# A fused convolution and RWKV-7 block: depthwise taps at the lowest priority, x normalised two tiles at once, side work in one queue per slot, h loaded ahead, the chunk chain traced later, the adaLN gate computed in block 1

## The chip, the cores and the metric

The kernel runs on one core of a Trainium2 chip. A core has TensorE (PE in the profile; its weight loads are PEld), VectorE (DVE), ScalarE (ACT), GpSimd (POOL) and SyncE (SP), which here only issues DMAs. Each engine works through its own queue in order and meets the others at semaphores. The metric is the device time of one execution, in microseconds.

## The reference, cut to what matters

```python
mod = silu(c) @ ada_w + ada_b;  shift, scale, gate = split(mod, 3)
h = rmsnorm(x, norm_g) * (1 + scale) + shift                       # 2048 tokens x 1024
p = h @ w_in                                                       # 1024 x 9344, split in the next line
c_val, c_gate, c_og, ts, r_og, g_conv, g_rwkv = split(p)

u = c_val * sigmoid(c_gate)
u = causal_depthwise_conv(u, conv_k, width=31) + conv_b            # per channel, along the tokens
y_conv = (silu(layernorm(u)) * silu(c_og)) @ w_conv_out

r, k, v, w_low, a_low = split(token_shift(ts, mu))                 # 16 heads of 64
decay, a = f(w_low @ w2), sigmoid(a0 + a_low @ a2)
for t in tokens:                                                   # per head, state S is 64 x 64
    S = S * decay[t] - (S @ kk[t]) b[t]^T + v[t] k[t]^T;  o[t] = S @ r[t]
o = groupnorm(o) + sum(r * k * r_k) * v
y_rwkv = (o * silu(r_og)) @ w_rwkv_out

m = sigmoid(g_conv) * y_conv + sigmoid(g_rwkv) * y_rwkv
out = rmsnorm(x + gate * (m @ w_out), final_g)
```

All is float32. `gate` enters only at the end; `shift` and `scale` are needed for the first h.

## The kernel before

The 2048 tokens are worked in four blocks of 512 (b = 0 to 3). Channels lie on partitions. A projection is one 128-channel tile of `w_in`: `mm3` makes it of 24 matmuls (8 slices of D, and three products each of the high and low parts of weight and h, since a float32 is split in two parts for PE's faster float32 form). These matmuls, at L180, are called main matmuls. A block projects 73 such tiles: one for the low-rank parts (`lora_split`) and then 18 in each of four slots. A slot (b, g) belongs to group g, which is two pairs of heads times two, 256 channels: `slot` projects k, r, v for each pair, and between and after them convolution and gate tiles (`fill`). 432 main matmuls make a slot.

Beside this stream run side tasks, written as Python generators. A task's `yield a, b` says that what it just emitted takes PE a us and that it goes on b us later; `tick` counts 0.684 us for every three main matmuls and polls the tasks. So PE's order, which is kept as written (`manual_schedule`), has the tasks' matmuls at planned places between main matmuls. `drain` lets the planned time run on without main matmuls until a task is done. The other engines' queues and SP's are ordered by the Tile scheduler from a simulated timeline, with priorities (`tc.high_priority`); its order is fixed in the program. The tasks are:

- `pair`: for one pair, decay, the chunk matrices `KR`, `BK`, the masked products `As` (PE L569, mask on DVE L572 and L579), transposes `tk`.
- `group`: when both pairs of a slot have their `As`, the 64x64 triangles are inverted: 32x32 quarters go out by DMA (`dA`, `La`), POOL does 62 small operations (L653, L655: "the inverse"), the result comes back (`dT`), DVE transposes quarters (L687), PE makes the lower and upper quarters (L700, L704). Then the chunk chain: 8 chunks of 64 tokens with three PE steps each (L757, then DVE `Xz`; L766, then DVE `uv`; L782, then the state `S` on DVE, L786). Then the group norm (DVE L803 to L811, POOL L805 and L812, ACT L808), and for each pair four PE transposes (L819) into the one PSUM bank `late`, which ACT empties (`oc`, L821). The chain of slot g runs while slot g+1 projects.
- `taps`: the 31 taps of one convolution tile on DVE (L861, L866), summed in one PSUM bank.
- `xnorm`: token tiles (128 tokens) of x for the next block: squares on ACT, a reciprocal root by some ten 128x1 operations on DVE (`rsqrt`, L109 to L114), x scaled (L365), transposed on PE (L371), modulated on ACT and stored as `xT_dram`. `XN` says which tiles a slot takes: here one in slot 0, one in slot 1, two in slot 2.

`hprep` reads h of the next block from `xT_dram`, tile by tile, and splits it in a high (ACT L384) and a low part (DVE L385). `presplit` splits a half tile of `w_out` (named "o": row gate from DRAM, multiplied on POOL, L144) or of `w_rwkv_out` ("ro") in two parts (ACT L145, POOL L146) and stores them; four such halves are emitted at the start of each slot of blocks 1 (w_out) and 2 (w_rwkv_out). The gate column is made after slot (0,0) by eight loads of 512 KB and DVE products (`ada_cols`, L200, L201), and its row goes to DRAM (L1039). Small tiles of all these share seven buffers, `hx`. In block 3 the LayerNorm of block 0 (`lnorm_first`) is done in three parts. After the blocks follow the output projections, block by block, with LayerNorm and final norm (L1087 to L1209).

## Time and profile before

| what | us |
|---|---|
| median of 3 runs (lowest, highest) | 3078.06 (3073.18, 3084.10) |
| the profiled execution, its own time | 3076.14 |
| its span, first to last instruction | 3074.4 |
| TensorE matmul, busy in the span | 2806.0 |
| VectorE, GpSimd, ScalarE busy | 2092.9, 1183.6, 1003.0 |

How to read it: `L371` is line 371 of the kernel before; `out<-in` are the names of the tiles an instruction writes and reads. In a list of waits stand the total us, how often, and the longest. In a window's row stand its length, each engine's busy us with the number of instructions (PE, PEld, DVE, ACT, POOL), the granted share of TensorE's clock, the DMA engines' busy share and GB/s. In a timeline, start and us, then the instruction, and in brackets how long the engine was idle before it and what ended that. In a list of groups, us in total and mean ns of one, then idle time before them.

### The profile page before, as it was taken

How to read it: one execution, taken by the hardware profiler on the slowest of the kernel's cores; microseconds unless marked ns; L12 is line 12 of the kernel's file. 1: busy time of each engine (PE TensorE's matmuls, PEld its weight loads, DVE VectorE, ACT ScalarE, POOL GpSimd, SP SyncE). 2: the span in 40 equal slices, each digit the busy share in tenths (PEclk: the TensorE clock that was granted, in tenths of full speed). 3: DMA queues.
4: the chain of work that ended last, by engine and by line, in shares of the span. 5: the costliest groups of instructions: out<-in, count | busy, mean ns of one | idle time of the engine just before them, and what ended most of it. 6: DMA issues, size and time to landing. Idle time of an engine off the chain costs nothing.

```text
span 3074.4 us, 50973 instructions
## 1 busy us (share of the span) xinstructions
PE 2806.0 (91%) x18640; PEld 2292.0 (75%) x18640; DVE 2092.9 (68%) x4279; ACT 1003.0 (33%) x1932; POOL 1183.6 (38%) x1742
## 2 busy tenths in 40 slices
...
GB/s 305 271 233 200 233 226 258 199 248 173 194 198 204 194 243 159 209 170 216 176 211 220 185 169 263 208 210 171 227 199 153 256 189 293 305 250 240 217 225 177
DMA packets 354795, 666.90 MB, mean 217 GB/s; under 512 B 134704, under 2 KB 153456, under 8 KB 354544
## 3 DMA queue, kind: packets, MB, share of 16 engines
...
q8 instruction: 147, 2.41, 0.3%
q14 instruction: 104, 0.85, 0.1%
HBM read 483.07 MB, written 179.31 MB: 215 GB/s over the span
## 4 chain that ended last, share of the span: by engine, by line
PE 40%; DVE 15%; DMA 8%; POOL 6%; issue 4%; SPq 2%; ACT 1%; POOLq 0%; DVEq 0%; ACTq 0%
PE ps_main L180 27%; DVE acc L866 5%; PE pout L1187 2%; PE pout L1186 2%; PE pout L1188 2%; DMA w_st<-w_ro_t 1%; POOL TT L655 1%; POOL itmp L653 1%; PE aux L569 1%; DMA w_gr<-grow_d 1%; PE xo L766 1%; SPq L666 1%; PE xo L740 1%; DVE S L786 1%; PE xo L782 1%
## 5 line engine op out<-in xcount | busy, mean ns | idle before, releaser
L180 PE MATMUL ps_main<-h_hi,w_hi 128*128 128x512 f32 x2304 | 966.3, 419 | 27.1 <-ACT w_hi L163 14.5
L180 PE MATMUL ps_main<-h_hi,w_lo 128*128 128x512 f32 x2304 | 918.9, 399 | 12.4 <-DMA w_lo<-kl_in 4.8
L180 PE MATMUL ps_main<-h_lo,w_hi 128*128 128x512 f32 x2304 | 915.6, 397 | 0.2 <-DVE h_lo L385 0.2
L866 DVE SCALAR_TENSOR_TENSOR acc<-u,ck,acc 128x512 f32<-128x512 f32 x928 | 697.9, 752 | 21.0
L180 PEld LDWEIGHTS ps_main<-h_hi,w_hi 128*128 128x128 f32 x2304 | 442.5, 192 | 121.5 <-ACT w_hi L163 16.4
L180 PEld LDWEIGHTS ps_main<-h_hi,w_lo 128*128 128x128 f32 x2304 | 440.2, 191 | 120.7 <-POOL w_lo L165 7.6
L180 PEld LDWEIGHTS ps_main<-h_lo,w_hi 128*128 128x128 f32 x2304 | 442.7, 192 | 80.1 <-DVE h_lo L385 1.4
L653 POOL TENSOR_TENSOR itmp<-La,TT 128x126 f32<-128x126 f32 (+22 forms) x496 | 181.9, 367 | 156.4 <-DMA La<-dA 120.5
L786 DVE SCALAR_TENSOR_TENSOR S<-xo,pe,Se 64x64 f32<-64x64 f32 x512 | 144.7, 283 | 141.9 <-PE xo L782 129.4
L163 ACT CAST w_hi<-w_st 128x1024 fp32r<-128x1024 f32 x103 | 108.0, 1048 | 307.2 <-DMA w_st<-w_in_t 128.1
L655 POOL TENSOR_TENSOR TT<-TT,itmp 128x126 f32<-128x126 f32 (+22 forms) x496 | 190.9, 385 | 35.3
L165 POOL TENSOR_TENSOR w_lo<-w_st,w_hi 128x1024 fp32r<-128x1024 f32 x50 | 120.5, 2409 | 133.0 <-ACT w_hi L163 58.2
L761 ACT ACTIVATE Se<-S,pe 128x128 f32<-128x128 f32 x256 | 89.0, 395 | 142.9 <-DVE S L786 141.9
L766 PEld LDWEIGHTS xo<-Xz,As 128*64 128x64 f32 x1024 | 69.6, 138 | 70.4 <-DVE Xz L762 38.4
L165 DVE TENSOR_TENSOR w_lo<-w_st,w_hi 128x1024 fp32r<-128x1024 f32 x53 | 70.5, 1331 | 68.0 <-PE ps_main L180 38.3
L572 DVE TENSOR_TENSOR As<-aux,maskA 128x512 f32<-128x512 f32 x128 | 82.7, 684 | 47.5 <-PE aux L569 47.0
L450 ACT ACTIVATE t<-ps_main,mu 128x512 f32<-128x512 f32 x96 | 65.9, 686 | 136.5 <-PE ps_main L180 133.9
L735 ACT COPY Xz<-xo 64x256 f32<-64x256 f32 x128 | 46.9, 367 | 189.4 <-PE xo L740 129.6
L766 PE MATMUL xo<-Xz,As 128*64 128x64 f32 x1024 | 87.4, 229 | 23.2 <-DVE Xz L762 23.0
L777 DVE TENSOR_TENSOR uv<-xo,rn 64x256 f32<-64x256 f32 x128 | 53.7, 419 | 80.3 <-PE xo L766 66.6
L847 POOL COPY u<-tail 128x30 f32<-128x30 f32 x32 | 10.2, 322 | 251.5 <-DVE yj L866 237.7
L762 DVE TENSOR_TENSOR Xz<-xo,Xz 64x256 f32<-64x256 f32 x128 | 53.7, 420 | 77.4 <-PE xo L757 75.8
...
## 6 DMA issues: line engine op xcount, KB each, us to landing
w_hi<-kh_in SPq DMA_DIRECT2D x219, 512.0 KB, 3.9
w_lo<-kl_in SPq DMA_DIRECT2D x219, 512.0 KB, 5.1
...
```

What stands on the lines that cost most here:

```text
L163: nc.scalar.copy(hi, st)
L165: lo_eng.tensor_tensor(out=lo, in0=st, in1=hi.bitcast(F32), op=ALU.subtract)
L180: nc.tensor.matmul(ps[:, qs], ww[:, k, :], aa[k][:, qs], start=(k == 0 and t == 0 and q == 0), stop=(k == KT - 1 and t == 2 and q == ms - ...
L450: nc.scalar.activation(t1, ps, AF.Identity, scale=mu1[:, mi:mi + 1])
L572: nc.vector.tensor_tensor(out=Asb[:, hh, c4 * 4:c4 * 4 + 4, :].rearrange("p (a e) n -> p a (e n)", e=2), in0=pA[hh], in1=flat(maskA).unsqu ...
L653: nc.gpsimd.tensor_tensor(out=tmp[:, :ni, :nt], in0=La[:, j:j + 1, j + 1:].broadcast_to([P, ni, nt]), in1=TT[:, :ni, j:j + 1].broadcast_to ...
L655: nc.gpsimd.tensor_tensor(out=TT[:, :ni, j + 1:], in0=TT[:, :ni, j + 1:], in1=tmp[:, :ni, :nt], op=ALU.add)
L761: nc.scalar.mul(Se[:, q, :], Sg[:, q, :], R[q]["pe"][:, c:c + 1])
L766: nc.tensor.matmul(b_[pr_, q, hs], As[q][:, hh, c, kcol(e)], Xz[:, e, q, hs], start=(n == 0), stop=(n == 3), skip_group_check=True)
L786: nc.vector.scalar_tensor_tensor(out=Sg[hs, q, hs], in0=b_[hs, 2 + q, hs], scalar=R[q]["pe"][hs, c:c + 1], in1=Se[hs, q, hs], op0=ALU.mult ...
L866: nc.vector.scalar_tensor_tensor(out=acc if i + 1 < HALO else yj, in0=u[:, i:i + TB], scalar=ck[:, j, i:i + 1], in1=acc, op0=ALU.mult, op1 ...
L1186: nc.tensor.matmul(o_, mhi[kk][:, ts_], whi[:, k, :], start=first, stop=False, skip_group_check=True)
```

## The change

- `taps`: each tap is emitted at a priority of -1500 (`LOWP`).
- `xnorm`: slot 0 takes two tiles, slot 1 the other two. Both tiles are loaded, squared and scaled first, their small DVE operations at high priority; after a longer planned delay (8 + 28 us for one tile's 18) follow the transposes.
- `sides`: one task per slot does, one after another, `xnorm`, then in slot (1,0) the gate (`gate_col`), in block 3 a part of the LayerNorm (`norms`), and in blocks 1 and 2 four presplits, 4 us apart. The list `later` is turned round: `w_rwkv_out` in block 1, `w_out` in block 2, since its row gate is made in block 1 now.
- `gate_col`: 16 loads of 256 KB into `hx` buffers, each with a DVE product, and the row to DRAM; `ada_cols` for the gate after slot (0,0) is gone.
- `hload`: h of the next block is loaded (seven tiles in `hx`, one in the buffer of `sq`) before the last three tiles of slot 3; `hprep` only splits.
- `pair` and `group` have longer planned delays: in `pair` 4.5 for 3.0, 6.0 for 4.5, 3.0 for 2.6; before the quarters 6.0 for 4.5; the chain's three steps 2.6 for 2.0, 2.5 for 2.0, 3.3 for 2.8; the norm, now at high priority, 30 for 18 us before its transposes.

```diff
@@ -45,9 +45,10 @@
-
-XN = ((0,), (1,), (2, 3), ())
+LOWP = 1500
+
+
+XN = ((0, 1), (2, 3), (), ())
 ZN = ((0, 1, 2), (3, 4, 5), (6, 7), ())
@@ -127,7 +128,7 @@
 
     kept = {}
 
-    later = [("o", (cb, kh)) for cb in range(4) for kh in range(2)] + [("ro", j) for j in range(KT)]
+    later = [("ro", j) for j in range(KT)] + [("o", (cb, kh)) for cb in range(4) for kh in range(2)]
...
 
     def xnorm(b, tts):
+        if not tts:
+            return
+        held = []
         for tt in tts:
...
             for half in range(2):
                 xt = hx("xt")
                 nc.sync.dma_start(xt, x[t0:t0 + P, half * TB:half * TB + TB])
-                nc.scalar.activation(hx("xsq"), xt, AF.Square, accum_out=ss[:, half:half + 1])
                 xh.append(xt)
+            for half in range(2):
+                nc.scalar.activation(hx("xsq"), xh[half], AF.Square, accum_out=ss[:, half:half + 1])
             vs, rs = ss[:, 2:3], ss[:, 3:4]
-            nc.vector.tensor_tensor(out=vs, in0=ss[:, 0:1], in1=ss[:, 1:2], op=ALU.add)
-            nc.vector.tensor_scalar(out=vs, in0=vs, scalar1=1.0 / D, scalar2=RMS_EPS, op0=ALU.mult, op1=ALU.add)
-            rsqrt(rs, vs, e2, nc.vector, ss[:, 4:5])
-            for kh in range(2):
-                nc.vector.tensor_scalar(out=xh[kh], in0=xh[kh], scalar1=rs, scalar2=None, op0=ALU.mult)
-            yield 0.0, 18.0
+            with tc.high_priority(HP):
+                nc.vector.tensor_tensor(out=vs, in0=ss[:, 0:1], in1=ss[:, 1:2], op=ALU.add)
+                nc.vector.tensor_scalar(out=vs, in0=vs, scalar1=1.0 / D, scalar2=RMS_EPS, op0=ALU.mult, op1=ALU.add)
+                rsqrt(rs, vs, e2, nc.vector, ss[:, 4:5])
+                for kh in range(2):
+                    nc.vector.tensor_scalar(out=xh[kh], in0=xh[kh], scalar1=rs, scalar2=None, op0=ALU.mult)
+            held.append((tt, xh))
+            yield 0.0, 8.0
+        yield 0.0, 28.0
+        for tt, xh in held:
             for kh in range(2):
                 yield free
                 pt = pl.tile([P, 4, P], F32, name="late", tag="late")
@@ -375,7 +384,7 @@
                     nc.scalar.activation(xo[:, i, :], pt[:, i, :], AF.Identity, scale=g_col[:, k:k + 1],
                                          bias=shift_col[:, k:k + 1])
                 nc.sync.dma_start(xT_dram[b][:, kh * 4:kh * 4 + 4, tt * P:(tt + 1) * P], xo)
-                yield 0.6, 3.5
+                yield 0.6, 4.5
 
...
 
-    def hprep(b):
+    def hload(b):
+        hfs = []
+        for k in range(KT):
+            hf = hx("hf") if k < HXB else e1.tile([P, TB], F32, name="hf", tag="sq")
+            nc.sync.dma_start(hf, xT_dram[b][:, k, :])
+            hfs.append(hf)
+        return hfs
+
+    def hprep(hfs):
         h = ([], [])
         for k in range(KT):
-            hf = hx("hf")
-            nc.sync.dma_start(hf, xT_dram[b][:, k, :])
-            hsplit(h, k, hf)
+            hsplit(h, k, hfs[k])
         return h
...
                                            scalar=vc("rwkv_k_k", pr), in1=E1x[:, :, e, :], op0=ALU.mult, op1=ALU.mult)
-        yield 0.0, 3.0
+        yield 0.0, 4.5
         yield free
...
-        yield 0.0, 4.5
+        yield 0.0, 6.0
...
-            yield 1.2, 2.6
+            yield 1.2, 3.0
...
-        yield 0.0, 4.5
+        yield 0.0, 6.0
...
-            yield 0.6, 2.0
+            yield 0.6, 2.6
...
-            yield 1.1, 2.0
+            yield 1.1, 2.5
...
-            yield 0.6, 2.8
+            yield 0.6, 3.3
...
-        yield 0.5, 18.0
+        with tc.high_priority(HP):
+            nc.vector.tensor_reduce(out=r4(st), in_=O16, axis=AX.X, op=ALU.add)
+            nc.vector.tensor_scalar(out=st, in0=st, scalar1=1.0 / 64, scalar2=None, op0=ALU.mult)
+            nc.gpsimd.tensor_tensor(out=O16, in0=O16, in1=bc(st), op=ALU.subtract)
+            for half in range(2):
+                Dm = lt.tile([P, 8, 64], F32, name="Dm", tag="oc", bufs=OCB)
+                nc.scalar.activation(Dm.rearrange("p (a b) n -> p a b n", a=2), O16[:, half * 2:half * 2 + 2], AF.Square)
+                nc.vector.tensor_reduce(out=st[:, half * 8:half * 8 + 8], in_=Dm, axis=AX.X, op=ALU.add)
+            nc.vector.tensor_scalar(out=st, in0=st, scalar1=1.0 / 64, scalar2=GN_EPS, op0=ALU.mult, op1=ALU.add)
+            rsqrt(rs, st, lt, nc.vector)
+            nc.gpsimd.tensor_tensor(out=O16, in0=O16, in1=bc(rs), op=ALU.mult)
+        yield 0.5, 30.0
...
-        nc.vector.tensor_scalar(out=acc, in0=u[:, HALO:], scalar1=ck[:, j, HALO:HALO + 1], scalar2=vc("conv_b", j),
-                                op0=ALU.mult, op1=ALU.add)
+        with tc.high_priority(-LOWP):
+            nc.vector.tensor_scalar(out=acc, in0=u[:, HALO:], scalar1=ck[:, j, HALO:HALO + 1], scalar2=vc("conv_b", j),
+                                    op0=ALU.mult, op1=ALU.add)
         for i in range(HALO):
             if i % 2:
                 yield 0.0, 2.0
-            nc.vector.scalar_tensor_tensor(out=acc if i + 1 < HALO else yj, in0=u[:, i:i + TB],
-                                           scalar=ck[:, j, i:i + 1], in1=acc, op0=ALU.mult, op1=ALU.add)
+            with tc.high_priority(-LOWP):
+                nc.vector.scalar_tensor_tensor(out=acc if i + 1 < HALO else yj, in0=u[:, i:i + TB],
+                                               scalar=ck[:, j, i:i + 1], in1=acc, op0=ALU.mult, op1=ALU.add)
...
-    def once(f):
-        yield free
-        f()
+    def gate_col():
+        sr = []
...
+        hg = e2.tile([P, 2, KT], F32, name="hg", tag="hg", bufs=1)
+        yield 0.0, 3.0
+        for k in range(KT):
+            for half in range(2):
+                st_ = hx("ada")
+                nc.sync.dma_start(st_, ada[16 + k][:, half * TB:half * TB + TB])
+                nc.vector.scalar_tensor_tensor(out=st_, in0=st_, scalar=1.0, in1=sr[half], op0=ALU.mult, op1=ALU.mult,
+                                               accum_out=hg[:, half, k:k + 1])
+            yield 0.0, 3.0
+        nc.vector.tensor_tensor(out=hgate_col, in0=hg[:, 0, :], in1=hg[:, 1, :], op=ALU.add)
+        nc.vector.tensor_tensor(out=hgate_col, in0=hgate_col, in1=ab[:, 16:24], op=ALU.add)
+        nc.vector.tensor_scalar(out=hgate_col, in0=hgate_col, scalar1=0.5, scalar2=None, op0=ALU.mult)
+        nc.sync.dma_start(grow_d.rearrange("(n p) -> p n", p=P), hgate_col)
+
+    def sides(b, g):
+        if b + 1 < NB:
+            yield from xnorm(b + 1, XN[g])
+        if b == 1 and g == 0:
+            yield from gate_col()
+        yield from norms(b, g)
+        if b in (1, 2):
+            for _ in range(2):
+                n_ = later.pop(0)
+                for half in range(2):
+                    presplit(*n_, half)
+                    yield 0.0, 4.0
+
+    def norms(b, g):
+        if b + 1 == NB and g < 3:
+            yield free
+            lnorm_first(g)
...
@@ -981,16 +1037,9 @@
         G = opened(b, g, h, lora)
         if first:
             G.wait = 8.0
-        if b in (1, 2):
-            for _ in range(2):
-                n_ = later.pop(0)
-                for half in range(2):
-                    presplit(*n_, half)
-        if b + 1 < NB:
-            side[:] = [Task(xnorm(b + 1, XN[g]))]
-        else:
+        side[:] = [Task(sides(b, g))]
+        if b + 1 == NB:
             z_first(ZN[g])
-            side[:] = [Task(once(lambda: lnorm_first(g)))] if g < 3 else []
...
+        if g < 3 or b + 1 == NB:
+            fill(len(todo))
+            return None
+        fill(len(todo) - 3)
+        drain(*side)
+        hfs = hload(b + 1)
         fill(len(todo))
+        return hfs
...
     with tc.manual_schedule(engines={mybir.EngineType.PE}):
         for b in range(NB):
             if b:
-                drain(*side)
-                h = hprep(b)
+                h = hprep(hfs)
             lora = lora_split(h)
             for g in groups:
-                slot(b, g, h, lora, g == 0)
-                if b == 0 and g == GG:
-                    for _ in ada_cols(srow, l3, "As", ASB, [((16 + k, 17 + k), (hgate_col[:, k:k + 1], hgate_col[:, k + 1:k + 2]))
-                                                            for k in range(0, KT, 2)]):
-                        pass
-                    nc.vector.tensor_tensor(out=hgate_col, in0=hgate_col, in1=ab[:, 16:24], op=ALU.add)
-                    nc.vector.tensor_scalar(out=hgate_col, in0=hgate_col, scalar1=0.5, scalar2=None, op0=ALU.mult)
-                    nc.sync.dma_start(grow_d.rearrange("(n p) -> p n", p=P), hgate_col)
+                hfs = slot(b, g, h, lora, g == 0)
         drain(*pairs_, *convs)
 
```

Three places in the engines' orders. DVE at the start of slot (1,0), with `acc` a tap, `ss` a step of the reciprocal root, `xt` a half tile of x; before:

```order
L866 SCALAR_TENSOR_TENSOR acc<-u,ck,acc 128x512 x3
L786 SCALAR_TENSOR_TENSOR S_426<-xo,pe,Se 64x64 x4
L866 SCALAR_TENSOR_TENSOR acc<-u,ck,acc 128x512 x15
L361 TENSOR_TENSOR ss<-ss 128x1
L866 SCALAR_TENSOR_TENSOR acc<-u,ck,acc 128x512
L362 TENSOR_SCALAR ss<-ss 128x1
```

and now:

```order
L367 TENSOR_TENSOR ss<-ss 128x1
L368 TENSOR_SCALAR ss<-ss 128x1
L110 TENSOR_SCALAR ss<-ss 128x1
L113 TENSOR_TENSOR ss<-ss 128x1
L114 SCALAR_TENSOR_TENSOR ss<-ss 128x1
L733 COPY As<-late 32x8x32 x2
L115 SCALAR_TENSOR_TENSOR ss<-ss 128x1
L733 COPY As<-aux 32x8x32 x2
```

The first step moved from behind 18 taps of the slot's first convolution to ahead of all of them, and ahead of the copies of `As` that end the triangles; before, each step had one tap between it and the next.

PE where a group's transposes stand, with `late<-ident,uv` a pair's four and `aux<-lw,wl` the next slot's first matmul; before, near the end of slot (1,2):

```order
L180 MATMUL ps_main<-h_hi,w_lo 128x512
L819 MATMUL late<-ident,uv 128x128 x4
L180 MATMUL ps_main<-h_hi,w_hi 128x512
L180 MATMUL ps_main<-h_lo,w_hi 128x512
L180 MATMUL ps_main<-h_hi,w_lo 128x512
```

and now, at the start of slot (1,2):

```order
L181 MATMUL ps_main<-h_hi,w_lo 128x512
L835 MATMUL late<-ident,uv 128x128 x8
L510 MATMUL aux<-lw,wl 128x512
L511 MATMUL aux<-lw,wlo 128x512
L515 MATMUL aux<-la,wl 128x512
L516 MATMUL aux<-la,wlo 128x512
```

The two pairs' transposes were 12 main matmuls apart inside a slot; now they stand side by side at the start of the next one. The chain's last step stood at main matmul 267 to 336 of a slot and stands at 306 to 396, in most slots at 315, and the transposes that begin the quarters at main matmul 24 of a slot, where they stood at 30 to 69.

POOL at the end of the inverse of slot (2,1), with `itmp` and `TT` the inverse, `w_st` and `w_lo` a presplit, `uv<-` the clearing of the next slot's tile; before, a stretch of that inverse:

```order
L653 TENSOR_TENSOR itmp<-La,TT 128x13x7
L655 TENSOR_TENSOR TT<-TT,itmp 128x13x7
L653 TENSOR_TENSOR itmp<-La,TT 128x13x6
L655 TENSOR_TENSOR TT<-TT,itmp 128x13x6
L653 TENSOR_TENSOR itmp<-La,TT 128x14x5
```

and now:

```order
L670 TENSOR_TENSOR TT<-TT,itmp 128x13x7
L145 TENSOR_TENSOR w_st<-w_st,w_gr 128x512
L828 TENSOR_TENSOR uv<-uv,grs 128x4x256
L668 TENSOR_TENSOR itmp<-La,TT 128x13x6
L147 TENSOR_TENSOR w_lo<-w_st,w_hi 128x512
L670 TENSOR_TENSOR TT<-TT,itmp 128x13x6
L668 TENSOR_TENSOR itmp<-La,TT 128x14x5
L634 MEMSET uv 64x4x256
```

Seven row-gate products (`w_st`), seven low parts (`w_lo`), the norm's last operation and two clearings stand between the inverse's first and last operation now. 

18 lines of the change are left out of this document (8 added, 10 removed).

## The prediction

> **What bounds the kernel now.** First the page's head, then each slot as a window, then what TensorE (PE) waited for, and only then single places in the timelines of the engines that it waited for.
>
> ```profile
> span 3074.4 us, 50973 instructions
> ...
> PE 2806.0 (91%) x18640; PEld 2292.0 (75%) x18640; DVE 2092.9 (68%) x4279; ACT 1003.0 (33%) x1932; POOL 1183.6 (38%) x1742
> ```
>
> PE carries the time: 2806.0 of 3074.4 us, so some 268 us are idle, and no other engine comes near. The change leaves PE's matmuls as they are, hence all that it can win or lose is that idle time (and a little clock). Where it lies is told by the busy time of windows, one to a slot (a block's quarter; the windows begin at a slot's first main matmul): length, then PE's busy time.
>
> ```profile
> 188.50:356.70 168.20, 141.97 (x965) 112.58 (x964) 112.98 (x236) 62.60 (x111) 84.25 (x110) 0.93 0.68 223
> ...
> 667.50:838.80 171.30, 139.61 (x969) 112.35 (x968) 102.10 (x226) 52.91 (x109) 65.43 (x104) 0.91 0.61 197
> 838.80:982.60 143.80, 137.29 (x965) 111.27 (x964) 97.98 (x219) 45.36 (x95) 55.85 (x102) 0.98 0.63 194
> ...
> 1269.20:1435.00 165.80, 140.42 (x969) 113.38 (x968) 108.62 (x231) 52.31 (x109) 55.06 (x96) 0.91 0.61 198
> 1435.00:1580.40 145.40, 138.07 (x965) 111.28 (x964) 98.95 (x219) 45.60 (x95) 51.42 (x98) 0.98 0.59 189
> ...
> 2299.30:2437.80 138.50, 134.17 (x953) 109.02 (x951) 98.90 (x206) 39.43 (x79) 41.36 (x82) 0.99 0.56 184
> ```
>
> The first slots of blocks 1 and 2 idle 31.7 and 25.4 us (171.30 - 139.61, 165.80 - 140.42), slot (0,1) 26.2, while the slots after them idle 6.5 and 7.3 and the last one 4.3. So the loss is not spread: it sits in a few places. The waits of PE (total, times, longest) name them.
>
> ```profile
> PE late L371 <- DVE xt L365: 49.4, 2, 27.7
> PE xo L766 <- DVE Xz L762: 23.0, 22, 3.0
> PE ps_main L180 <- DVE mr L1100: 18.5, 2, 15.9
> PE late L819 <- POOL uv L812: 18.3, 3, 10.9
> ...
> PE ps_main L180 <- ACT h_hi L384: 12.2, 3, 5.3
> PE aux L533 <- ACT sq L525: 9.9, 7, 4.7
> ...
> PE aux L569 <- POOL KR L552: 6.8, 5, 2.3
> PE xo L782 <- DVE uv L777: 6.7, 7, 3.7
> ```
>
> **The change, part by part.** The sum is made against the profiled execution, 3076.1 us (span 3074.4), 1.9 under the median of 3078.06.
>
> *x normalised for two tiles, its VectorE work early.* The two waits at L371 are 49.4 us. VectorE's timeline shows why:
>
> ```profile
> 690.10 11.84 DVE L866 SCALAR_TENSOR_TENSOR acc<-u,ck,acc 128x512 f32<-128x512 f32 x15
> 706.54 0.16 DVE L361 TENSOR_TENSOR ss<-ss 128x1 f32<-128x1 f32 x1 [4.60 <-ACT xsq L358]
> ...
> 715.44 0.88 DVE L365 TENSOR_SCALAR xt<-xt,ss 128x512 f32<-128x512 f32 x2
> ```
>
> Fifteen taps run first, x itself comes late (4.60 us of waiting for the squares), and then each tiny step of the reciprocal root stands behind a tap, up to 715.44, when PE goes on. In the new order the tiny steps stand ahead of the taps, and PE's transposes come at main matmul 141 of the slot rather than 63. The wait goes. What is late next: the first small step still waits for x, and now stands ahead of the As copies that let the chunk chain begin; I take 2 us in each of two blocks, bounded by 0 and by the 7 that both 4.60 waits would leave. Term: -45 (-49 to -42).
>
> *The adaLN gate leaves block 0.* Between 150 and 215 us, right after the gate's eight 512 KB loads, PE waits for weights:
>
> ```profile
> PE ps_main L180 <- ACT w_hi L163: 14.0, 3, 5.9
> PE ps_main L180 <- POOL w_lo L165: 3.7, 3, 1.4
> ```
>
> That is 17.7 us; other slots of block 0 split weights too and are not wholly free of it, so -15. In block 1 sixteen 256 KB loads come instead, nine of them on SP's queue between two pairs of weight loads, and sixteen more VectorE operations stand among the steps of a chunk chain. Weights are prefetched two projections ahead there, and taps are absent from that stretch, so most is hidden; no row shows the rest. Between 0 and the 17.7 that the same bytes cost in block 0 I take 6, nearer 0 because these weights need no split. Term: -9 (-18 to +3).
>
> *h loaded ahead.* The three waits for h_hi are 12.2 us, at the starts of blocks 1 to 3. The loads now land while the last projections run, and the cast of a tile can only begin when the last projection has freed the old one, as before. Term: -10 (-12 to 0).
>
> *Group norm and its transposes.* Of the 18.3 us at L819, 10.9 lie at the end of slot (0,1), whose chain still ends late; the other 7.4 go. But the two pairs' transposes now stand next to each other at every slot's start, as they did once:
>
> ```profile
> 352.11 1.11 PE L819 MATMUL late<-ident,uv 128*128 128x128 f32 x4 [10.85 <-POOL uv L812]
> 354.10 1.12 PE L819 MATMUL late<-ident,uv 128*128 128x128 f32 x4 [0.87 <-ACT oc L821]
> ```
>
> Both write one PSUM bank, and the second waits for ScalarE to empty it: 1.99 us from start to start, some 0.8 of it matmul, so 1.2 lost. Thirteen slots have this newly: +16 (0 to 26 if all of 1.99 were lost). Term with the 7: +9. It rests on the norm being done in time. The next rows are, of a late slot, the last state update on VectorE, the norm's last operation on POOL (both from timelines), and a stretch of the chain that ended last:
>
> ```profile
> 2259.12 1.18 DVE L786 SCALAR_TENSOR_TENSOR S<-xo,pe,Se 64x64 f32<-64x64 f32 x4 [2.84 <-PE xo L782]
> 2274.00 1.91 POOL L812 TENSOR_TENSOR uv<-uv,grs 128x1024 f32<-128x1024 f32 x1 [0.17 <-DVE grs L114]
> 2263.08 18.74 PE ps_main L180 x81
> ```
>
> From the last state update (ends 2260.3) to the norm's end (2275.9) it is 15.6 us, and 81 main matmuls take 18.74, 0.231 each. A regular chain now ends at main matmul 315 of 432, 117 ahead of the transposes: 27 us.
>
> *The chain traced later.* Three main matmuls more stand ahead of a chunk's second and third step (12 for 9), 0.69 us each. The waits for Xz and uv (23.0 and 6.7, 29 times) can lose 20; those for the squares and KR (9.9 and 6.8, 12 times), whose delays grow by 1.5 us, about 10. I take -28 (0 to -46, the sum of the four).
>
> *One queue of side work per slot.* The presplit of `w_out` (each half: POOL L144, then L146) moves to block 2 behind the normalisation, and in slot (2,1) it falls into the triangular inverse. The rows are, of that slot, the mask's last operation, the inverse's first and last, PE's first use of it (timelines), and three groups of POOL's with their mean ns:
>
> ```profile
> 1523.71 1.41 DVE L579 TENSOR_TENSOR As<-As,rn 64x512 f32<-64x512 f32 x2
> 1536.11 0.24 POOL L653 TENSOR_TENSOR itmp<-La,TT 128x31 f32<-128x31 f32 x1 [4.02 <-DMA La<-dA]
> 1564.94 0.29 POOL L655 TENSOR_TENSOR TT<-TT,itmp 128x16 f32<-128x16 f32 x1
> 1588.10 0.21 PE L700 MATMUL late<-T,As 32*32 32x32 f32 x1
> L146 POOL TENSOR_TENSOR w_lo<-w_st,w_hi 128x512 fp32r<-128x512 f32 x32 | 41.3, 1292 | 66.4 <-ACT w_hi L145 66.3
> L619 POOL MEMSET uv<- 64x1024 f32 x32 | 30.4, 949 | 26.2 <-PE late L819 18.5 <-PE ps_x L421 6.5
> L144 POOL TENSOR_TENSOR w_st<-w_st,w_gr 128x512 f32<-128x512 f32 x16 | 20.8, 1303 | 73.8 <-DMA w_gr<-grow_d 73.8
> ```
>
> Before, the inverse took 29.1 us here (1536.1 to 1565.2), and PE began the blocks' lower quarters 63.0 after the mask was ready (1525.1 to 1588.1). Now seven L144 (9.1), seven L146 (9.0), a norm operation that stood behind it (1.9, above), two L619 (1.9) and small ones (1.6) stand inside: 52.6. Around the inverse the path needs at least 24 (10 until `La` is there, 8 for the way back, 4 for the transposes, the rest issue), so 77 against the 61 that PE now gives (15 fewer main matmuls than before, less the new pair of transposes): a wait of 16. L144 can add waits for its row (73.8 us over 16 in the old place), and the end could slip less; 0 to 35. In slot (1,2) VectorE's transposes stand behind a pair's first operations: +3. Term: +19.
>
> *Clock.* PE's busy time is 2.3 us more in the first slots of blocks 1 and 2 than in the next ones (139.61 against 137.29, 140.42 against 138.07) at a granted 0.91 against 0.98: work done at the lower clock after a long idle stretch. Two such stretches go, with five shorter ones (two for weights, two for h, one at L819) that I price at half; one long one comes in (2,2): -2.3 x 2 - 1.15 x 5 + 2.3 = -8, with the short waits for h in slot (1,0) -9 (-15 to 0). The Trainium skill ("TensorE: Matmul & The Clock Gate", Part 1) lets the clock fall to half after an idle window of about 3.4 us and rise again after as long a busy one, so the thirteen new waits of 1.2 us would leave it up, and each long one costs half of 3.4; by that figure seven gone and one come are an estimated -10, and the sum would be 1 us lower.
>
> *At nothing:* taps at the lowest priority. In a steady slot they stand among the same neighbours as before; they are covered by VectorE's 30% of idle time, and without that cover a slot would pay for a tap (0.75 us) in each chain step. *The tail:* the 15.9 us at L1100 come from VectorE's row scaling behind the LayerNorm of block 1; the new order puts the scaling first, but the last chain ends 87 main matmuls later and pushes that LayerNorm towards its own use. I take 0 (-15 to +15).
>
> Sum: -45 - 9 - 10 + 9 - 28 + 19 - 9 + 0 = -73, so 3003 in the profiled run and 3005 as a median.
>
> **The rivals.**
> - *The norm is late at every slot's start.* One mechanism: POOL's L812 is in PE's way 13 times. It decides from 27 us between the chain's end and the norm's end; each us more costs 13. For it: the norm's operations have two inputs in SBUF and run beside POOL, and the following rows show such 128x1 operations at 0.65 us each (1.35 for two, overlapping) while POOL runs long ones, and at 0.12 without.
>
> ```profile
> 2621.74 1.35 DVE L113 SCALAR_TENSOR_TENSOR rs_t<-rs_t,vs 128x1 f32<-128x1 f32 x2
> 2642.03 0.23 DVE L113 SCALAR_TENSOR_TENSOR rs_t<-rs_t,vs 128x1 f32<-128x1 f32 x2
> ```
>
>   If twelve such steps each waited for a whole operation of 1.3 us on POOL, 15.6 + 15.6 = 31.2, hence 4 us late; with POOL's own queue (a 1.9 and a 1.3 ahead of L812) 7 late, 13 x 7 = 91, or 3005 + 91 = 3096. Against it: POOL's neighbours there are inverse steps of 0.4 us. The Trainium skill ("SBUF — State Buffer", "Who interferes with whom") has the shared port taken as a lock for a whole instruction, which is this mechanism; these two rows agree with it. Chance 0.13.
> - *SP's queue pays for the gate and the presplits.* The 17.7 us return in block 1, the inverse of (2,1) costs 35 and h gains nothing: 3005 + 12 + 19 + 10 = 3046. Chance 0.11.
> - *The normalisation is moved but x is not there.* If x lands as late as at 706.54 and now holds up VectorE's queue ahead of the chain, the two waits return in another place: 3005 + 45 + 9 (no clock gain) = 3059; with two slow chains on top, no change. Chance 0.08, of which 0.05 lie within 0.3%.
>
> **How the numbers follow.** My forecast has 0.68. Half-widths of the terms (4, 11, 6, 13, 23, 18, 8, 15), unrelated, add to 40 (root of the squares), 2965 to 3045. The whole range reaches up to the second and third rival: 2958 to 3062. 0.3% of 3078 is 9 us, about what a measurement of this kernel can tell from no change. Faster: 0.68 + 0.11 + 0.03 = 0.82; same 0.05; slower 0.13.
>
> **What would show it.** In the new profile the wait at the x transposes should be under 5 us in all; the first slots of blocks 1 and 2 about as long as the slots after them (some 145 to 150 us); waits for w_hi in the first 215 us under 5; no wait for h_hi over 2; at L819's successor thirteen waits of about 1 us for ScalarE's oc, none long but that of slot (0,2); a wait of 10 to 20 us for the transposes ahead of the inverse's quarters in slot (2,2). I am wrong if PE waits for POOL's norm at slot starts, if slot (1,0) stays over 160 us, or if the last 640 us grow by more than 15.

## The result and the profile after

The changed kernel takes 3054.97 us in the median of four runs (3053.94 to 3056.81), beside 3077.48 for the kernel before; the ratio is 0.9926, 95% interval 0.9907 to 0.9944. The time is inside the range that was given, but the gain is 22.5 us where 73 had been forecast, less than a third of it. The profiled run took 3055.97 us.

The page's head first, and then windows that begin at a slot's first main matmul, of slots (0,1), (1,0), (2,0), (2,1), (2,2) and (3,3). In each window: length, then busy us and instructions of PE, PEld, DVE, ACT, POOL, the granted clock, the DMA share and GB/s.

```profile
span 3054.2 us, 50967 instructions
...
PE 2818.2 (92%) x18640; PEld 2294.3 (75%) x18640; DVE 2099.5 (69%) x4300; ACT 1001.7 (33%) x1934; POOL 1186.5 (39%) x1742
```

```profile
180.34:357.48 177.14, 147.40 (x973) 116.98 (x972) 118.11 (x231) 65.11 (x116) 86.76 (x118) 0.90 0.70 231
...
655.13:816.07 160.94, 143.61 (x980) 113.82 (x978) 122.25 (x300) 57.15 (x123) 54.02 (x93) 0.97 0.67 222
...
1247.11:1397.55 150.44, 140.95 (x979) 113.17 (x978) 114.22 (x265) 55.31 (x121) 55.22 (x97) 0.98 0.67 212
1397.55:1552.93 155.38, 139.43 (x973) 112.30 (x972) 101.38 (x207) 50.62 (x107) 69.91 (x105) 0.95 0.70 224
1552.93:1708.68 155.75, 138.04 (x958) 111.52 (x956) 96.08 (x208) 40.04 (x81) 52.11 (x106) 0.93 0.53 169
...
2279.68:2413.11 133.43, 132.49 (x949) 107.19 (x947) 94.62 (x200) 38.24 (x78) 42.63 (x84) 1.00 0.59 198
```

PE is busy for 12.2 us more than before (2818.2 against 2806.0), and the span is 20.2 shorter, so idle time fell by 32.4 us and a good third of that came back as busy time. The first slots of blocks 1 and 2 are 10.4 and 15.4 us shorter; slots (2,1) and (2,2), which took 145.41 and 142.45, are 10.0 and 13.3 longer. What PE waited for (total, times, longest):

```profile
PE late L835 <- POOL uv L828: 30.9, 4, 14.5
PE late L715 <- DVE T L702: 29.4, 5, 14.9
PE xo L781 <- DVE Xz L777: 17.9, 11, 3.5
...
PE late L835 <- ACT oc L837: 14.6, 14, 1.3
PE ps_main L181 <- DVE mr L1148: 12.1, 3, 6.9
PE ps_main L181 <- ACT w_hi L164: 9.3, 3, 4.8
```

The wait at the x transposes, 49.4 us, is gone from the head of the list. At its head stand the group's transposes (L835), for the norm on GpSimd and for ScalarE, and the quarters behind the triangular inverse (L715). The two largest places, from PE's timeline:

```profile
1548.33 1.12 PE L835 MATMUL late<-ident,uv 128*128 128x128 f32 x4 [11.62 <-POOL uv L828]
...
1574.49 0.28 PE L715 MATMUL late<-T,As 32*32 32x32 f32 x2 [14.86 <-DVE T L702]
```

Both come from the presplits of `w_out` in slot (2,1). GpSimd's timeline of that slot, with the row-gate product of a presplit and the last operation of the norm:

```profile
1508.98 1.27 POOL L145 TENSOR_TENSOR w_st<-w_st,w_gr 128x512 f32<-128x512 f32 x1 [2.37 <-DMA w_gr<-grow_d]
...
1545.15 1.26 POOL L145 TENSOR_TENSOR w_st<-w_st,w_gr 128x512 f32<-128x512 f32 x1 [3.16 <-DMA w_gr<-grow_d]
1546.37 1.90 POOL L828 TENSOR_TENSOR uv<-uv,grs 128x1024 f32<-128x1024 f32 x1
```

GpSimd stands waiting for rows from DRAM (2.37 and 3.16 us here) with the inverse and the norm queued behind. The inverse took 61.3 us (1499.1 to 1560.4) where 52.6 had been forecast, and the norm 37.2 from the chain's last state update.

### The profile page after: what moved, and what is told of

It is laid out like the page before. It is cut to its first block, busy times and chain, and to the rows that moved or that the text cites. A ratio compares the mean times of both kernels' runs of the same rounds, so it can differ in the third digit from the quotient of the medians.

```text
span 3054.2 us, 50967 instructions
## 1 busy us (share of the span) xinstructions
PE 2818.2 (92%) x18640; PEld 2294.3 (75%) x18640; DVE 2099.5 (69%) x4300; ACT 1001.7 (33%) x1934; POOL 1186.5 (39%) x1742
## 4 chain that ended last, share of the span: by engine, by line
PE 45%; DVE 26%; DMA 13%; issue 6%; POOL 5%; ACT 3%; SPq 3%; POOLq 0%; DVEq 0%; ACTq 0%
PE ps_main L181 32%; DVE acc L884 8%; DMA w_st<-w_in_t 2%; DVE M L521 1%; PE pout L1235 1%; PE pout L1236 1%; PE pout L1234 1%; DVE S L801 1%; DMA w_gr<-grow_d 1%; PE xo L781 1%; PE aux L584 1%; PE xo L797 1%; PE xo L755 1%; DMA w_lo<-kl_in 1%; PE xo L772 1%
## 5 line engine op out<-in xcount | busy, mean ns | idle before, releaser
L623 POOL TENSOR_TENSOR vv<-rk,vv 128x512 f32<-128x512 f32 x32 | 41.3, 1290 | 188.8 <-PE aux L620 134.5
L781 PE MATMUL xo<-Xz,As 128*64 128x64 f32 x1024 | 88.2, 230 | 19.1 <-DVE Xz L777 17.9
```

The costliest lines, as they stand in the source:

```text
L781: nc.tensor.matmul(b_[pr_, q, hs], As[q][:, hh, c, kcol(e)], Xz[:, e, q, hs], start=(n == 0), stop=(n == 3), skip_group_check=True)
```

## The experiments

Ratios are against the kernel before on the same chip in the same job; its median there is 3075.9 to 3081.9 us, so times of two jobs compare less well than ratios. Runs of one kernel lie a few us apart for most, and up to 20 for one; a difference under some 8 us between two kernels of this table tells little. Nor is a difference always made where the edit is: from the last main matmul to the end, where the code of the output is the same in all, the traces of the eighteen kernels take 630 to 649 us.

| kernel | us (lowest to highest) | ratio to before, 95% |
|---|---|---|
| changed | 3055.0 (3053.9 to 3056.8) | 0.9926 (0.9907, 0.9944) |
| before + two-tile normalisation (a_xnorm) | 3052.4 (3050.5 to 3055.2) | 0.9905 (0.9890, 0.9920) |
| before + presplits behind x (a_sides) | 3047.1 (3041.4 to 3049.8) | 0.9895 (0.9877, 0.9913) |
| changed, old normalisation (u_xnorm) | 3055.7 (3054.5 to 3059.2) | 0.9923 (0.9901, 0.9944) |
| changed, presplits first (u_presplit) | 3054.4 (3051.3 to 3054.9) | 0.9921 (0.9906, 0.9936) |
| changed, both undone (u_both) | 3076.5 (3069.5 to 3081.5) | 0.9998 (0.9983, 1.0013) |
| changed, old chain delays (u_chain) | 3057.4 (3049.4 to 3063.0) | 0.9919 (0.9897, 0.9940) |
| changed, old pair delays (u_pair) | 3047.3 (3042.4 to 3051.5) | 0.9893 (0.9868, 0.9917) |
| changed, taps at normal priority (u_taps) | 3047.4 (3044.2 to 3052.9) | 0.9896 (0.9872, 0.9919) |
| changed, gate in block 0 (u_gate) | 3054.8 (3051.3 to 3063.7) | 0.9923 (0.9907, 0.9939) |
| changed, h loaded late (u_hload) | 3057.0 (3049.3 to 3059.9) | 0.9922 (0.9892, 0.9953) |
| changed, second bank (v_bank) | 3029.7 (3026.3 to 3033.6) | 0.9833 (0.9817, 0.9850) |
| changed, presplits held (v_dep) | 3047.0 (3037.6 to 3057.8) | 0.9888 (0.9862, 0.9914) |
| v_bank with presplits held, other slot (v_best1) | 3023.2 (3020.1 to 3029.0) | 0.9818 (0.9804, 0.9833) |
| v_bank, old pair delays, normal taps (v_mix1) | 3041.8 (3030.5 to 3043.9) | 0.9875 (0.9853, 0.9896) |
| changed + 16 short stalls (s_short) | 3070.6 (3065.0 to 3072.3) | 0.9967 (0.9954, 0.9980) |
| changed + 16 longer stalls (s_long) | 3094.6 (3092.5 to 3098.1) | 1.0052 (1.0035, 1.0068) |

### What the whole gain is

One part alone, put into the kernel before (its `xnorm` and `XN` replaced by the changed ones):

```diff
-XN = ((0,), (1,), (2, 3), ())
+XN = ((0, 1), (2, 3), (), ())
...
+    yield 0.0, 28.0
```

> The kernel before with one part of the change alone: x normalised two tiles at once, with the small VectorE steps at high priority and the longer delay. Theory 'this part is the whole gain and more': the 49 us of waits at the x transposes go, but the presplits, now behind more tiles of the shared buffers, fall into an inverse in block 1 (ten POOL operations of 1.3 us): 3078 - 49 - 3 (clock) + 14 = 3040 us (3030 to 3050). Rival 'the stall only moves' (to the chain's copies of As and to the first pair): 3055 to 3070.

It took 3052.4: this part alone is worth as much as the whole change. The other way round, the changed kernel with the normalisation as before:

> The changed kernel with the normalisation of x as before (one, one and two tiles in slots 0, 1 and 2, a delay of 18 us, its small VectorE steps at normal priority). Theory 'the two-tile normalisation wins its 49 us of waits and gives part back, because it pushes the presplits into the inverse of (2,1)': the x waits return (49 and 4 for the clock), the 28 us at (2,1) and (2,2) and 5 of clock go: 3055 + 53 - 33 = 3075 us (3065 to 3085). Rival 'the two are independent': 3108 us.

It took 3055.7, so undoing the same part costs nothing. Neither theory had that: 3052.4 lies between the two ranges given for the first kernel, and 3055.7 under both of the second. The reason was in its waits, the row of the x transposes, here L372:

```profile
PE late L372 <- DVE xt L366: 9.4, 2, 6.7
```

The old normalisation waits 9.4 us there and not 49.4. So the long stall had another cause than the prediction's, and something else in the change had cured it too. VectorE's timeline of that kernel in slot (1,0) shows that it isn't the taps:

```profile
679.65 0.16 DVE L362 TENSOR_TENSOR ss<-ss 128x1 f32<-128x1 f32 x1 [2.56 <-ACT xsq L359]
679.72 0.75 DVE L876 SCALAR_TENSOR_TENSOR acc<-u,ck,acc 128x512 f32<-128x512 f32 x1
680.38 0.15 DVE L363 TENSOR_SCALAR ss<-ss 128x1 f32<-128x1 f32 x1
680.50 0.76 DVE L876 SCALAR_TENSOR_TENSOR acc<-u,ck,acc 128x512 f32<-128x512 f32 x1
...
690.25 0.88 DVE L366 TENSOR_SCALAR xt<-xt,ss 128x512 f32<-128x512 f32 x2
```

The taps have the lowest priority there, and still one stands between every two steps: 10.6 us from the first step to the scaling, 8.9 in the kernel before (706.54 to 715.44). What moved is the first step: 18 us behind the slot's first main matmul (661.5), and 39 before (667.5). SP's queue of the kernel before tells why, in slot (1,0):

```profile
672.79 0.54 SPq L139 DMA_DIRECT2D w_st<-w_o_t  x1
...
693.91 0.42 SPq L139 DMA_DIRECT2D w_st<-w_o_t  x1
...
700.33 0.32 SPq L148 DMA_DIRECT2D kh_o<-w_hi  x1
700.70 0.42 SPq L357 DMA_DIRECT2D xt<-x_in  x1
```

Four presplits, each with its loads, its wait for a buffer and its stores, stand ahead of the first load of x, which goes out 33 us into the slot. In the changed kernel the normalisation comes first in the queue of side work, and x goes out 7 us into the slot (662.17 against 655.13). Only blocks 1 and 2 have presplits, and only there the stall was. Three more kernels complete the square of old and new normalisation with old and new order. The first has only the order, put into the kernel before:

```diff
-        if b in (1, 2):
-            for _ in range(2):
...
-                    presplit(*n_, half)
-            side[:] = [Task(xnorm(b + 1, XN[g]))]
+            side[:] = [Task(queue(b, g))]
...
+    def queue(b, g):
+        yield from xnorm(b + 1, XN[g])
+        if b in (1, 2):
...
+                    presplit(*n_, half)
+                    yield 0.0, 4.0
```

> The kernel before with one part of the change alone: in blocks 1 and 2 the presplits come behind the normalisation of x in the side task, 4 us apart, instead of ahead of it at the slot's start; the normalisation itself, the taps and all delays as before. Theory 'x came late because four presplits stood ahead of its loads on SP's queue' (before, the loads of x stand on SP 33 us into slot (1,0), at 700.7): the waits at the x transposes fall from 49 to under 12 us, 3080 - 38 = 3042 us (3035 to 3056). Rival, the prediction's reading 'the small VectorE steps stand behind taps': the waits stay above 30 us, 3068 to 3082.

The second undoes both in the changed kernel, and the third the order alone:

```diff
+        if b in (1, 2):
+            for _ in range(2):
...
+                    presplit(*n_, half)
         side[:] = [Task(sides(b, g))]
```

(and `sides` loses its own).

> The changed kernel with both undone: the normalisation of x as before, and the presplits at the slot's start ahead of it. Theory 'either of the two cures the stall at the x transposes': without both it is back, 40 us or more of waits and 3 of clock over the 3056 us of the run with the old normalisation behind the new queue: 3096 us (3085 to 3105). Rival 'the taps at the lowest priority had cured it': 3052 to 3062.

> The changed kernel with the presplits at the slot's start ahead of the normalisation, which stays as changed. Theory 'either of the two cures the stall': its delay of 36 us covers the late loads, waits at the x transposes under 12 us, 3058 us (3050 to 3068). Rival 'only the order of the loads cures it': 3085 or more.

The waits at the x transposes, of the order alone and of the kernel with both undone:

```profile
PE late L371 <- DVE xt L365: 10.3, 2, 5.9
```

```profile
PE late L372 <- DVE xt L366: 53.3, 2, 30.1
```

| normalisation, order | presplits first | x first |
|---|---|---|
| as before | 3076.5 (waits 53.3) | 3055.7 (9.4) |
| two tiles, longer delay | 3054.4 (9.5) | 3055.0 (1.5) |

Either cures the stall: the order brings x earlier, the delay lets PE come later. With both undone the stall is back, though the time of 3076.5 is under the 3085 to 3105 that the theory gave. With neither, all the other parts of the change together are worth nothing: ratio 0.9998 (0.9983, 1.0013). So the gain is the stall's, and the rest of the change adds up to zero.

### Why 50 us of waits are worth 22

In the kernel with both undone the first slots of blocks 1 and 2 take 181 and 176 us, and 161 and 150 with the change: 46 less. Slots (2,1) and (2,2) take 142 and 140 there, and 155 and 156 with the change: 29 more. SP's queue shows what fills them. Of the sixteen presplits of `w_out` four have their loads in slot (2,1) with both undone, and eleven in the changed kernel (from 1458 to 1548). Presplits and x share the `hx` buffers; the old normalisation loads its last tile of x in slot (2,2) (1602 us), ahead of the last presplits, while the new one is done with x in (2,1) (last store at 1463 us), and the presplits of slots (2,2) and (2,3) follow at once. Fourteen of their operations fall into the inverse of (2,1). The other traces agree: four such loads in (2,1) with the old normalisation and the new order, eight with the new normalisation and the presplits first. To take them out of the inverse, they were made to depend on the chain:

```diff
+            if b == 2 and g in (1, 2) and c == 0:
+                for hh in range(2):
+                    hs = slice(64 * hh, 64 * hh + 64)
+                    nc.vector.scalar_tensor_tensor(out=hgate_col[hs], in0=Sg[hs, 0, 64 * hh:64 * hh + KT], scalar=0.0,
+                                                   in1=hgate_col[hs], op0=ALU.mult, op1=ALU.add)
+                nc.sync.dma_start(grow_d.rearrange("(n p) -> p n", p=P), hgate_col)
+                quart[0] = g + 1
...
-        if b in (1, 2):
-            for _ in range(2):
+        if b == 1 or (b == 2 and g > 1):
+            if b == 2:
+                yield lambda: quart[0] == g
+            for _ in range(2 * b):
```

> The changed kernel, with the sixteen presplits of w_out held until a group's chain has begun, eight in slot (2,2) and eight in (2,3), so that none stands in a triangular inverse of block 2 (a new small write of the gate's row after the chain's first chunk is what they wait for). Theory 'POOL pile-up': the 14.9 and 1.6 us at the quarters of slot (2,2), the 11.6 at the transposes behind slot (2,1) and the half-clock stretches of 14 and 20 us around them go; slots (2,1) and (2,2) fall from 155.4 and 155.7 to 143 to 145 each; 3030 us (3025 to 3036). Rival 'the change's longer chain is what is late there': the slots stay above 150, 3048 to 3058.

Slot (2,1) fell to 137 us and the waits of 11.6 and 14.9 us are gone, as the theory said, but (2,2) stayed at 152 and (2,3) rose from 140 to 165; 3047.0 in all, just under the rival's range. The presplits' price moved with them. Its waits for a pair's work on ScalarE (behind GpSimd) and for the chain:

```profile
PE xo L781 <- DVE Xz L777: 28.0, 13, 5.2
...
PE aux L610 <- ACT tk L605: 9.9, 2, 5.0
```

### The transposes of the two pairs

```diff
-            po = pl.tile([P, NTT, P], F32, name="late", tag="late")
+            p_, n_ = ((pl, "late"), (pa, "aux"))[q]
+            po = p_.tile([P, NTT, P], F32, name=n_, tag=n_)
```

> The changed kernel, with the transposes of a group's second pair in the other PSUM bank (aux), so that they need not wait until ScalarE has emptied the first pair's. Theory 'one bank': the wait for oc, 14.6 us in 14 places, goes, nothing takes its place: 3041 us (3037 to 3046). Rival 'passed on': PE then waits as long for the aux bank or for the work behind the transposes: 3050 to 3058.

It took 3029.7, 25.3 us less than the changed kernel and below both ranges. The 14.6 us of waits are gone; 5.5 came back behind them:

```profile
PE aux L515 <- ACT oc L838: 5.5, 7, 1.6
```

Idle time fell by 16.1 us in the profiled runs and PE's busy time by 11.8: the trace's clock record has 27 stretches at half clock, 184 us, where that of the changed kernel has 32, 214 us. But not all of this is shown to be the bank's. Of the 27.9 us between the two spans 17.1 lie in the slots, which is near the 14.6 of the waits, and 12.3 behind the last main matmul, where no such wait stood and the other engines' queues came out in another order (the start is 1.5 longer). And of the fourteen waits in the changed kernel one alone, at 2133 us, began a half-clock stretch. So two transposes that a delay had brought side by side cost some 15 us; where the other 10 come from is open.

Both together, with the second half of the presplits in slot (3,3):

> The changed kernel with the second pair's transposes in the other bank and the sixteen presplits of w_out held until a chain has begun, eight in slot (2,2) and eight in (3,3), where GpSimd is idle most of the time, instead of eight in (2,3), where they took 25 us in the run before (165 for 140). Theory 'both losses add up': 3030 less the 18 to 25 that slots (2,1) and (2,2) gained, 3008 us (3000 to 3018). Rival 'held presplits cost a slot wherever they stand' (hx buffers and SP's queue): slot (3,3) grows from 133 to 150 or more, 3025 to 3035.

3023.2 us, ratio 0.9818, between the two ranges: faster than both kernels, though slot (3,3) grew from 133 to 148, near what the rival said, and slot (2,1) fell from 155 to 137. It is the fastest here.

### The delays, the taps, the gate and h

```diff
-            yield 0.6, 2.6
+            yield 0.6, 2.0
...
-            yield 1.1, 2.5
+            yield 1.1, 2.0
...
-            yield 0.6, 3.3
+            yield 0.6, 2.8
```

> The changed kernel with the three delays of the chunk chain as before (2.0, 2.0, 2.8), all else as changed. The idle time ahead of the chain's four PE steps was 34.9 us before and is 34.1 in the changed kernel. Theory 'the delays saved nothing, and a later chain meets more taps': waits ahead of the chain within 8 us of the changed kernel's, the norm shorter by 6 us in half of the slots, the pairs' transposes apart again in half of them (7 us less of waits for oc): 3048 us (3040 to 3056). Rival, the prediction's term 'each step's delay buys 0.69 us': waits ahead of Xz and uv rise by 15 to 20 us, 3066 (3060 to 3075).

The waits did what the rival said; the time, 3057.4, lies between the two ranges. Ahead of the chain PE waits 50 us with the old delays, where it waited 34; most of it:

```profile
PE xo L781 <- DVE Xz L777: 35.3, 30, 4.9
...
PE xo L772 <- DVE S L801: 9.4, 7, 3.1
...
PE xo L797 <- DVE uv L792: 4.4, 7, 1.1
```

So a longer delay does buy its 16 us. But the chain then ends later, and that costs: with the old delays the waits for the norm are 18.7 us and not 30.9, and those for the quarters 13.1 and not 29.4. The account does not close with these. With the old delays the waits for weights are 49 us and not 30, the slots take 17.5 us longer in the profiled run (3063.0, the slowest of the four), and the part behind the last main matmul takes 12.3 us less. Why the time is nearly the same is not shown.

```diff
-        yield 0.0, 4.5
+        yield 0.0, 3.0
...
-        yield 0.0, 6.0
+        yield 0.0, 4.5
...
-            yield 1.2, 3.0
+            yield 1.2, 2.6
```

> The changed kernel with the three delays in a pair as before (3.0, 4.5, 2.6), the chain's as changed. Idle time of PE ahead of a pair's steps was 31 us before and is 15 with the change. Theory 'here the longer delays did save': 3071 us (3063 to 3077). Rival 'as with the chain, whose old delays cost 2 us': 3051 to 3060.

The same again: with a pair's old delays its waits are 25 us instead of 15, and the time is 3047.3, not longer and below both ranges.

```diff
-LOWP = 1500
+LOWP = 0
```

> The changed kernel with the taps at normal priority. Theory 'the lowest priority does nothing, since VectorE's order was fixed by what is ready, and a tap always is': 3055 us (3051 to 3059), 10 us of waits ahead of Xz still behind a tap. Rival 'it keeps taps out of the chain': 3063 us or more.

3047.4, 7.6 us less than with the lowest priority and below both ranges. Of VectorE's 4300 operations 4239 stand in the same order, so no cause is claimed; a gain by the lowest priority does not show. PE still waits behind a tap in the changed kernel; VectorE at the chain's step in slot (2,0), where PE waited 3.5 us:

```profile
1280.63 0.74 DVE L555 SCALAR_TENSOR_TENSOR BK<-y,hkk,E 128x512 f32<-128x512 f32 x1
1281.29 0.74 DVE L884 SCALAR_TENSOR_TENSOR acc<-u,ck,acc 128x512 f32<-128x512 f32 x1
1281.95 0.41 DVE L777 TENSOR_TENSOR Xz<-xo,Xz 64x256 f32<-64x256 f32 x1
```

Of 19.1 us of PE's idle time at such steps 10.8 have a tap as VectorE's operation just ahead.

```diff
-        if b == 1 and g == 0:
-            yield from gate_col()
...
+                if b == 0 and g == 0:
+                    for _ in ada_cols(srow, l3, "As", ASB, [((16 + k, 17 + k), (hgate_col[:, k:k + 1], hgate_col[:, k + 1:k + 2]))
+                                                            for k in range(0, KT, 2)]):
+                        pass
...
```

> The changed kernel with the adaLN gate back behind slot (0,0) in eight loads of 512 KB, all else as changed. Theory 'moving the gate earned nothing': slots (0,0) and (0,1) take 294 us together with the change and took 292 before, and slot (1,0) takes 161 where its neighbours take 145; gate back gives +8 in block 0 and -10 in slot (1,0): 3053 us (3046 to 3060). Rival, the prediction's term of -9 and its clock share: 3064 to 3070.

3054.8: nothing, as the theory said. Slot (0,0) takes 135 us instead of 117, (0,1) 168 instead of 177, (1,0) 152 instead of 161, which is +18 - 9 - 9.

```diff
-        drain(*side)
-        hfs = hload(b + 1)
...
-                h = hprep(hfs)
+                drain(*side)
+                h = hprep(hload(b))
```

> The changed kernel with h loaded at the start of its block instead of ahead of the last three projections. Theory 'the prediction's term of 10 us stands': the waits for h at three block starts return, 12 us, and 3 of clock, 3070 us (3063 to 3076). Rival 'nothing': 3051 to 3059.

3057.0: nothing beyond the spread. But the waits for h did not return (0.2 us for its high part), since this kernel keeps what had removed them. In the kernel before, seven of the eight loads of block 1's h stand on SP's queue between 410 and 420 us, more than 230 us before the tiles are split; only the eighth, for which `hx` has no buffer left, goes out late, and ScalarE waits for it:

```profile
660.88 0.41 SPq L393 DMA_DIRECT2D hf<-xT  x1
...
665.07 0.62 ACT L384 CAST h_hi<-hf 128x512 fp32r<-128x512 f32 x1 [5.87 <-DMA hf<-xT]
```

`hload` puts the eighth tile in the buffer of `sq`. It goes out at 570 us in the changed kernel and at 562 in this one, and the other seven between 255 and 267 in both. So this run hardly moved a load, and no run shows what the eighth buffer earns.

The last one takes three of these together, to see whether the gains of 8 us are more than another order of the queues:

> The changed kernel with the second pair's transposes in the other bank, a pair's delays as before and the taps at normal priority, each of which was faster alone (25, 8 and 8 us). Theory 'they add': 3014 us (3008 to 3022). Rival 'the last two are the spread of one more order of the queues': 3024 to 3034.

3041.8, slower than the bank alone and above both ranges. The two gains of 8 us do not add, as the rival said; the waits for ScalarE behind the transposes, 5.5 us with the bank alone, are 16.3 here.

### The clock

```diff
             ps = project(h, ("in", ti + j))
+            if b in (1, 2) and j > 5 and free():
+                stl = e2.tile([P, TB], F32, name="stl", tag="t2", bufs=T2B)
+                pst = pl.tile([P, NTT, P], F32, name="late", tag="late")
+                with tc.high_priority(HP):
+                    nc.scalar.copy(stl[:, :128], ps[:, :128])
+                nc.tensor.transpose(pst[:, 0, :], stl[:, :P], ident)
```

> The changed kernel with sixteen short stalls of PE put into its two cleanest slots, (1,3) and (2,3), which have 1.4 us of idle time and no half-clock stretch: after each gate projection ScalarE copies 128x128 of the result and PE transposes the copy before it goes on. Both theories: some 0.9 us each, 16 x 0.9 + 16 x 0.1 = 16 us, no half-clock stretch in these slots, 3071 us (3066 to 3077).

> The same with two copies of 128x512, one after the other, at each of the sixteen places, so that PE waits about 2.2 us. Theory 'a stall of some 2 us already brings a half-clock stretch of 3.4 us': 16 x 2.2 = 35 us of idle time and 16 x 1.2 us lost at the lower clock, 3110 us (3100 to 3122), with ten or more half-clock stretches in the two slots. Rival, the prediction's clock term (an idle stretch under 3.4 us leaves the clock up): the idle time alone, 3090 us (3085 to 3095), no half-clock stretch.

The short stalls came out at up to 1.03 us, four of them without any idle time, and cost 15.6 us: 6.2 of idle time, 16 transposes of 0.33, and 4 more. Of these up to 3.4 are a wait of 1.70 us for a weight, 0.8 us behind a stall at 1237 us, and the half-clock stretch of 3.4 us that followed it; none had been expected in these slots. The longer ones (in the second kernel the copy is 128x512 and made twice) came out shorter than meant, 0.66 to 2.84 (27.4 us together), and cost 39.6. Two of them in PE's timeline, and windows of 6 us around each:

```profile
1145.79 0.33 PE L898 MATMUL late<-ident,stl 128*128 128x128 f32 x1 [2.36 <-ACT stl L897]
...
1228.47 0.33 PE L898 MATMUL late<-ident,stl 128*128 128x128 f32 x1 [1.80 <-ACT stl L897]
```

```profile
1144.00:1150.00 6.00, 4.21 (x13) 3.35 (x14) 5.86 (x15) 3.41 (x8) 0.97 (x2) 0.72 0.68 227
1227.00:1233.00 6.00, 4.53 (x20) 3.75 (x21) 5.82 (x10) 1.41 (x3) 1.91 (x1) 1.00 0.25 42
```

Behind 2.36 us idle the clock is 0.72 in the window, a stretch of 3.4 us at half; behind 1.80 it stays at 1.00. Of the five stalls of 2.25 us or more four brought such a stretch, of the eleven up to 1.94 none. That speaks for the theory's mechanism, while the time (3094.6) is in the rival's range: the stalls were shorter than meant, and four stretches came where ten had been expected.

## Why the prediction was wrong, step by step

The sign was right and the cause of the gain named at the right place; the size was wrong by 51 us. Row by row, idle time and clock come to some -24 for the forecast -73: 17 of the 49 between them lie at the norm and its transposes, 16 at the clock, 11 at the delays, and 4 each at the gate, the inverse and the tail, while x and h came out 5 and 2 better than forecast. (The clock's and the tail's rows overlap in part.)

| step of the sum | forecast | in the two traces, or by the runs |
|---|---|---|
| x normalisation | -45 | idle time there 51.2 to 1.5: -50; but 22 to 28 in time (u_both, a_xnorm) |
| gate, weights | -9 | idle for w_hi and w_lo 27 to 22: -5; time 0 (u_gate) |
| h ahead | -10 | waits -12; their time not shown (u_hload keeps the eighth buffer) |
| norm and transposes | +9 | idle time 19.3 to 45.5: +26; the bank alone 25, of which some 15 are the waits |
| chain and pair delays | -28 | chain 34.9 to 34.1, pair 31 to 15: -17 |
| inverse with presplits | +19 | 12 to 35: +23 |
| clock | -9 | half of PE's busy time at half clock 65.9 to 72.9: +7 |
| tail | 0 | window of the tail 636.6 to 641.1: +4 |

- *x normalised for two tiles.* The wait went as forecast. The step that failed is its cause, "fifteen taps run first": x was late, since four presplits stood ahead of it on SP's queue, and the taps filled the time. The idle 4.60 us behind those taps, in a row that the prediction quoted, said that x was what ended the wait. With the wrong cause it was not seen that the new order of side work alone cures the stall, nor that the presplits of the last two slots, with no tile of x ahead of them, move up into (2,1).
- *Group norm.* "From the last state update to the norm's end it is 15.6 us" was read in a slot without taps. In the changed kernel the chain ends where a convolution's taps run, and the norm takes 22 to 23 us in ten slots and 26 to 37 in five. Four rows of VectorE there:

```profile
2269.37 0.17 DVE L113 TENSOR_TENSOR rs_t<-grs 128x16 f32<-128x16 f32 x1
2269.49 0.76 DVE L884 SCALAR_TENSOR_TENSOR acc<-u,ck,acc 128x512 f32<-128x512 f32 x1
2270.16 0.17 DVE L114 SCALAR_TENSOR_TENSOR rs_t<-rs_t,gst 128x16 f32<-128x16 f32 x1
2270.28 0.76 DVE L884 SCALAR_TENSOR_TENSOR acc<-u,ck,acc 128x512 f32<-128x512 f32 x1
```

  The norm takes 23.0 us there. Its ten steps of the reciprocal root take 7.3 of them with a tap of 0.76 between any two, where they take 2.6 in the slot of the 15.6; the rest is work ahead of them, taps for the most part. The trace before had it: the same norm takes 22.2 us in slot (2,1). The norm stayed within the 27 us of room in most slots, so the first rival was wrong; but in (0,1), (0,2), (1,1) and (2,1), where the chain ends late or GpSimd is held up, PE waits 30.9. The wait of (0,1), 10.9 before, was forecast to stay; it became 14.5. The 1.2 us for the second pair were nearly right (14.6 in 14 places).
- *The chain traced later.* The delays do buy waits (16 us by the run with the old ones), but between the two traces the chain's idle time hardly fell (34.9 to 34.1). The term left out that a later chain can meet more taps, and that it ends closer to the norm's and the quarters' deadlines, where PE waits 12 and 16 us more than with the old delays. The first of these is argued from the waits behind taps, not shown by a run.
- *The gate* moved its cost from block 0 to slot (1,0), as the second rival said in its first part; the term's 9 us were not there.
- *h ahead.* The wait went as forecast, but the reading was wrong: the step "the loads now land while the last projections run" took all eight for late, and seven of them had landed more than 150 us earlier; only the eighth, for which `hx` had no buffer left, came late.
- *The inverse.* The wait in (2,2) was forecast at 16 and is 14.9 and 1.6; that in (1,2) at 3 and is 5.8 and 1.7.
- *Clock.* The step "Two such stretches go, with five shorter ones (...) that I price at half" let the price follow the idle time. That the short new waits leave the clock up was right for all but one. But PE has 30 stalls over 2 us before and 28 after, and the trace's clock record 30 and 32 half-clock stretches, though idle time fell by 32 us. The two long stretches that went (27.3 and 23.9 us) lay in stalls for the most part: PE was busy for 9.9 us in them. The Trainium skill ("TensorE: Matmul & The Clock Gate", Part 1) has the clock fall after an idle window of about 3.4 us; in the trace with the longer stalls four of five of 2.25 to 2.84 us were followed by half clock. The measurement decides.
- *Taps at the lowest priority at nothing:* right in that no gain came; by the run it may cost some us.

What the forecast said would show it: waits at x under 5 (1.5, right), no wait for h over 2 (right), waits for oc thirteen times about 1 us (14, right), no long wait for the norm but one (two, 14.5 and 11.6: wrong), 10 to 20 at the quarters of (2,2) (right), first slots of blocks 1 and 2 at 145 to 150 (161 and 150, half right), waits for w_hi under 5 in the first 215 us (4.8, right, with 8.1 more for w_lo). Of its signs of being wrong two came: PE waits for the norm in four places, and slot (1,0) takes 160.9 us. The half-widths of its terms add to 38.5 by their squares and not to 40, which changes nothing.

## What to carry to other kernels

Before a stall is put down to the operations that ran just ahead, ask when its input was sent for: follow the chain from the waiting engine through the DMA to the row on the issuing queue, and look what stands ahead of it there. A change of many parts is best priced by the square of its parts, done and undone: two parts may cure the same stall, so that each is worth the whole gain alone and nothing beside the other. A part that is undone must undo what removed the wait; the run with h loaded late kept the buffer that did. A later step in a hand-written order buys the wait ahead of it and can pay at the next deadline; price both. And stalls are to be counted as well as summed: one of 2.25 to 2.84 us brought 3.4 us of half clock in four cases of five.

## What the runs showed that had not been expected

- A stall of about 2 us is often enough for half clock. Over the 18 traces of this case, isolated stalls of PE (no other over 0.25 us within 9 us, and no half clock in the 9 us ahead) were followed within 3.6 us by a half-clock stretch of the clock record in 3 of 340 cases under 1.25 us, 12 of 68 from 1.25 to 1.75, 35 of 58 from 1.75 to 2.25, 49 of 65 from 2.25 to 3, and 95 of 99 above.
- The lowest priority does not keep a tap out of a chain of small dependent operations: in the rows of VectorE shown here one stands between every two, as in the kernel before.
- Putting the presplits behind x instead of ahead of it cost little in the slots behind (slots (1,2) and (1,3) take 6.2 and 4.4 us longer in the trace): the order alone, in the kernel before, is faster (0.9895) than all parts together (0.9926), though the intervals overlap.
